# Decoder trunk on one core: 1 MB weight tiles, wider casts and evictions, and a new layout of the split tokens

## The chip, the cores and the metric

The kernel runs on one core of a Trainium2 chip. The metric is the time of one execution on the device in microseconds (us). Before the change its median over three runs is 2126.35 us (2126.17 to 2127.8). One execution more was profiled; its trace is what the sections below read. TensorE, VectorE and ScalarE are called PE, DVE and ACT in the trace's rows, PEld is TensorE's loading of stationary operands, and SP issues the transfers of weights.

## The reference

Two decoder layers over 256 tokens of width 2048, all in fp32. The first layer mixes tokens with a sparse attention (an indexer of 16 small heads scores the keys, the best 64 are kept for each query, then 16 heads in 4 groups share 4 key/value heads), the second with an mLSTM of 8 heads. Each is followed by a feed-forward part (FFN) of width 8192 with a squared ReLU.

```python
for i in range(DEPTH):                       # 2
    hn = rms_norm(h, norm_mix[i])
    if i % N_MIXERS == 0:
        y = dsa_attention(hn, att_w_in[j], att_q_gain[j], att_k_gain[j], att_w_out[j])
    else:
        y = mlstm_mixer(hn, ml_w_in[j], ml_b_gate[j], ml_h_gain[j], ml_w_out[j])
    h = h + y
    hn = rms_norm(h, norm_ffn[i])
    h = h + jnp.square(jax.nn.relu(hn @ ffn_w_up[i])) @ ffn_w_down[i]
```

## The kernel before

Nearly all of the work is products of the 256 tokens with weights of 389 MB in total, each read once. To keep fp32's precision on a faster matmul, every operand is split into a high part (the value cast to the type fp32r) and a low part (the value less its high part), and a product is the sum of high x high, high x low and low x high. The split of a tile is `split` (L134 to 136): a cast on ScalarE (L135), then a subtraction on VectorE (L136).

`weights` (L138) brings four blocks of 128 weight rows, a *group*, against at most 512 columns, in two halves. For each half it takes a tile `w` (five of them), one transfer of 512 KB (L144), a tile `wh` and a tile `wl` (four each), and splits the 1024 columns. So there is room for two groups in wh and wl, in steps of half a group.

`project` (L152) puts the tokens on the stationary side and the weights on the moving side: 24 matmuls of 512 columns for a group, in the lines L166 (high, high), L167 (high, low) and L168 (low, high). It serves the attention's and mLSTM's projections and FFN down. `project_t` (L175) has the weights stationary and the tokens moving, so that the result comes out transposed: per block and 128 columns one matmul of the high weights with the tokens' high and low parts side by side (L191, 512 columns) and one of the low weights with the tokens' high parts (L193, 256 columns). It serves FFN up and the mLSTM's q and k. Its results lie alternately in the tiles `acc` and `acx`.

A `pair` (L60) holds the two parts of two blocks of tokens: [part][block][256 tokens]. L191 therefore reads two runs of 256 elements that lie 512 apart. Pairs are written by `Norm.chunk` (xT, L226 and L227), by the attention (oT), the mLSTM (hsT) and the eviction of FFN up (hT).

FFN runs in four quarters of 2048 hidden columns: four times `project_t` (512 columns each) and then four times `project`. The eviction `evac_up` of FFN up takes one block of 128 hidden columns at a time: a copy (L462), a sum (L463), max and square (L464) and a split, all 256 wide.

The attention projects V, the indexer, K and then Q in four head groups. The indexer's scores go through L355 and L360, the top-k through L366 and L367; in a head group the logits (L412, L417), exponentials (L422) and scalings (L427) make probabilities `lg`, which TensorE transposes (L434 to 436), ScalarE copies to `pT` (L438) and TensorE multiplies with V (L440, L442).

Nobody writes the order of the engines' instructions out by hand. The program names work in order of its stages, and a scheduler that plays the program through with its own estimates of durations gives each engine a fixed sequence when the kernel is built; a tile of a pool is handed on when its last reader is done. A changed size therefore changes the sequences too. The tile numbers in the sequences below are those of the build.

## Time and profile before

| what | value |
|---|---|
| median of three runs | 2126.35 us |
| span of the profiled execution | 2124.9 us |
| TensorE busy | 2115.0 us, 10748 matmuls |
| VectorE busy | 1242.6 us (58%), 1866 instructions |
| ScalarE busy | 1010.1 us (48%), 1400 instructions |
| read from memory | 389.16 MB, 184 GB/s over the span |
| mean granted clock of TensorE | 0.999 |

The stages follow one another: attention up to about 282 us and its output projection to 330, FFN of the first layer to 1034, mLSTM, and FFN of the second layer from about 1420 to the end. A quarter of an FFN takes 176 us. "Busy" on TensorE is from a matmul's start to its modelled end, and as matmuls overlap in the pipeline, their pace is read better from how many of them run in a stretch. A share of the chain that ended last says how much of the span went by on that chain in this line's work; what waits beside it costs nothing.

### The profile page before, as it was taken

The numbers are of one execution on the slowest core, as the hardware profiler recorded it, in microseconds if no ns is written. First come the engines' busy times: TensorE is split into PE (matmuls) and PEld (weight loads), VectorE is DVE, ScalarE is ACT, GpSimd is POOL, SyncE is SP. The second block draws the span as 40 slices with busy tenths as digits, with TensorE's granted clock in tenths as the row PEclk, the third lists the DMA queues.
The fourth block names the chain that finished last, engine by engine and source line by source line (L and its number), as shares of the span: only waits on it lengthen the run. The fifth ranks groups of instructions, "written<-read, shape, count | busy, mean of one in ns | idle before, by whom it ended". The sixth has DMA issues, their size and how long they took to land.

```text
span 2124.9 us, 27918 instructions
## 1 busy us (share of the span) xinstructions
PE 2115.0 (100%) x10748; PEld 1810.0 (85%) x10748; DVE 1242.6 (58%) x1866; ACT 1010.1 (48%) x1400; POOL 14.0 (1%) x20
## 2 busy tenths in 40 slices
PE   9999999999999999999999999999999999999999
PEld 8988888888888888888999888888888888888887
DVE  5697656645555565565654565656555555654654
ACT  6556554534443443444554554545434434443542
POOL 0000000000000000000011000000000000000000
PEclk9999999999999999999999999999999999999999
DMA  7665356656656656665566555466566666666664
GB/s 234 188 180 151 119 178 188 188 193 191 191 191 187 198 189 196 190 189 188 166 185 209 171 165 176 161 188 188 193 194 189 191 194 189 191 193 191 189 205 140
DMA packets 207926, 393.09 MB, mean 185 GB/s; under 512 B 12784, under 2 KB 29616, under 8 KB 207792
## 3 DMA queue, kind: packets, MB, share of 16 engines
q1 hardware_dynamic: 207744, 391.29, 60.4%
q8 instruction: 84, 1.38, 0.2%
q14 instruction: 50, 0.41, 0.1%
q10 hardware_dynamic: 48, 0.02, 0.0%
HBM read 389.16 MB, written 2.10 MB: 184 GB/s over the span
## 4 chain that ended last, share of the span: by engine, by line
PE 99%; ACT 0%; DMA 0%; DVE 0%; issue 0%; SPq 0%; DVEq 0%
PE acc L167 19%; PE acc L168 19%; PE acc L166 19%; PE acc L191 13%; PE acx L191 13%; PE acc L193 6%; PE acx L193 6%; PE aux L219 1%; PE aux L412 0%; PE aux L440 0%; PE aux L620 0%; PE aux L349 0%; DMA w<-in_att_w_in_dram 0%; PE aux L611 0%; PE aux L396 0%; PE aux L645 0%
## 5 line engine op out<-in xcount | busy, mean ns | idle before, releaser
L136 DVE TENSOR_TENSOR wl<-w,wh 128x1024 fp32r<-128x1024 f32 (+3 forms) x752 | 907.1, 1207 | 820.6 <-ACT wh L135 819.5
L135 ACT CAST wh<-w 128x1024 fp32r<-128x1024 f32 (+3 forms) x752 | 777.6, 1035 | 970.6 <-PE acc L168 576.6
L191 PE MATMUL acc<-xT,wh 128*128 128x512 f32 x1152 | 401.1, 394 | 0.0
L191 PE MATMUL acx<-xT,wh 128*128 128x512 f32 x1152 | 399.9, 393 | 0.0
L166 PE MATMUL acc<-wh,hT 128*128 128x512 f32 x1024 | 398.7, 389 | 0.0
L167 PE MATMUL acc<-wl,hT 128*128 128x512 f32 x1024 | 398.7, 389 | 0.0
L168 PE MATMUL acc<-wh,hT 128*128 128x512 f32 x1024 | 398.4, 389 | 0.0
L193 PE MATMUL acc<-xT,wl 128*128 128x256 f32 x1152 | 318.9, 278 | 0.0
L193 PE MATMUL acx<-xT,wl 128*128 128x256 f32 x1152 | 318.4, 278 | 0.0
L191 PEld LDWEIGHTS acx<-xT,wh 128*128 128x128 f32 x1152 | 215.7, 187 | 49.3
L191 PEld LDWEIGHTS acc<-xT,wh 128*128 128x128 f32 x1152 | 215.4, 188 | 48.9
L166 PEld LDWEIGHTS acc<-wh,hT 128*128 128x128 f32 x1024 | 192.2, 188 | 40.0
L168 PEld LDWEIGHTS acc<-wh,hT 128*128 128x128 f32 x1024 | 192.2, 188 | 39.7
L167 PEld LDWEIGHTS acc<-wl,hT 128*128 128x128 f32 x1024 | 192.2, 188 | 39.5
L193 PEld LDWEIGHTS acc<-xT,wl 128*128 128x128 f32 x1152 | 216.5, 188 | 1.3
L193 PEld LDWEIGHTS acx<-xT,wl 128*128 128x128 f32 x1152 | 216.2, 188 | 0.3
L166 PE MATMUL acc<-wh,xT 128*128 128x512 f32 (+3 forms) x576 | 212.4, 372 | 2.3 <-ACT xT L226 2.3
L167 PE MATMUL acc<-wl,xT 128*128 128x512 f32 (+3 forms) x576 | 212.7, 371 | 0.0
L168 PE MATMUL acc<-wh,xT 128*128 128x512 f32 (+3 forms) x576 | 211.9, 371 | 0.0
L166 PEld LDWEIGHTS acc<-wh,xT 128*128 128x128 f32 x576 | 108.1, 188 | 15.1 <-ACT xT L226 2.5
L167 PEld LDWEIGHTS acc<-wl,xT 128*128 128x128 f32 x576 | 108.3, 188 | 12.9 <-issue 0.7
L168 PEld LDWEIGHTS acc<-wh,xT 128*128 128x128 f32 x576 | 108.3, 188 | 12.8 <-issue 0.3
(204 smaller groups left out, 1308.1 us busy)
## 6 DMA issues: line engine op xcount, KB each, us to landing
w<-in_ffn_w_up_dram SPq DMA_DIRECT2D x256, 512.0 KB, 3.8
w<-in_ffn_w_down_dram SPq DMA_DIRECT2D x256, 512.0 KB, 4.3
w<-in_ml_w_in_dram SPq DMA_DIRECT2D x64, 512.0 KB, 3.8
w<-in_att_w_in_dram SPq DMA_DIRECT2D x48, 512.0 KB, 4.4
w<-in_att_w_out_dram SPq DMA_DIRECT2D x32, 512.0 KB, 4.4
w<-in_ml_w_out_dram SPq DMA_DIRECT2D x32, 512.0 KB, 3.7
w<-in_ml_w_in_dram SPq DMA_DIRECT2D x32, 412.0 KB, 3.7
w<-in_att_w_in_dram SPq DMA_DIRECT2D x24, 368.0 KB, 3.6
```

The source lines that it names most:

```text
L135: nc.scalar.copy(hi, src)
L136: nc.vector.tensor_tensor(lo, src, hi.bitcast(F32), op=ALU.subtract)
L166: nc.tensor.matmul(o, ah, wh[:, j, :width], start=(k == 0), stop=False)
L167: nc.tensor.matmul(o, ah, wl[:, j, :width], start=False, stop=False)
L168: nc.tensor.matmul(o, al, wh[:, j, :width], start=False, stop=(k == nk - 1))
L191: nc.tensor.matmul(acc[j], wh[:, kk % 2, js], a[:, :, k % 2], start=(k == 0), stop=False, skip_group_check=True)
L193: nc.tensor.matmul(acc[j][:, 1], wl[:, kk % 2, js], a[:, 0, k % 2], start=False, stop=(k == nk - 1), skip_group_check=True)
L219: nc.tensor.transpose(p[:, j * T + m * P:j * T + (m + 1) * P], h[:, m, k * P:(k + 1) * P], ident)
```

## The change

1. `weights` takes one tile `w` of 1 MB for a group (three of them), one transfer of 1 MB, one wh and one wl of 2048 columns (two of each), one cast and one subtraction. Only the first projection, whose tokens are made on the way (`before`), keeps two pieces, inside the same tiles.
2. A `pair` is laid out [block][part][256 tokens], so the moving operand of L191 is one run of 512; all writers and readers of pairs follow.
3. `evac_up` collects two blocks in `u` and then does max and square and the split for both at once, 512 wide, with a tile `y` more.
4. The attention has one tile `sq` (was two) and four `lg` (was five); two small mLSTM tiles share others' space. Comments and docstrings go.

```diff
@@ weights
-    def weights(src, k0, n0, width):
-        parts = []
-        for i in range(2):
-            w = wp.tile([P, 2, 512], F32, tag="w", name=uid("w"), bufs=5)
-            r0 = k0 + 256 * i
-            nc.sync.dma_start(w[:, :, :width], src[r0:r0 + 256, n0:n0 + width].rearrange("(k p) f -> p k f", p=P))
-            wh = wp.tile([P, 2, 512], F32R, tag="wh", name=uid("wh"), bufs=4)
-            wl = wp.tile([P, 2, 512], F32R, tag="wl", name=uid("wl"), bufs=4)
-            split(wh[:, :, :width], wl[:, :, :width], w[:, :, :width])
-            parts.append((wh, wl))
-        return parts
+    def weights(src, k0, n0, width, pieces=1):
+        w = wp.tile([P, 4, 512], F32, tag="w", name=uid("w"), bufs=3)
+        wh = wp.tile([P, 4, 512], F32R, tag="wh", name=uid("wh"), bufs=2)
+        wl = wp.tile([P, 4, 512], F32R, tag="wl", name=uid("wl"), bufs=2)
+        n = 4 // pieces
+        for i in range(pieces):
+            r0 = k0 + 128 * n * i
+            ks = slice(n * i, n * (i + 1))
+            nc.sync.dma_start(w[:, ks, :width],
+                              src[r0:r0 + 128 * n, n0:n0 + width].rearrange("(k p) f -> p k f", p=P))
+            split(wh[:, ks, :width], wl[:, ks, :width], w[:, ks, :width])
+        return wh, wl
@@ project
-            for i, (wh, wl) in enumerate(weights(src, k0 + 512 * g, n0, width)):
+            wh, wl = weights(src, k0 + 512 * g, n0, width, 1 if before is None else 2)
+            for i in range(2):
...
-                        ah, al = a[:, 0, j, ms], a[:, 1, j, ms]
-                        nc.tensor.matmul(o, ah, wh[:, j, :width], start=(k == 0), stop=False)
-                        nc.tensor.matmul(o, ah, wl[:, j, :width], start=False, stop=False)
-                        nc.tensor.matmul(o, al, wh[:, j, :width], start=False, stop=(k == nk - 1))
+                        ah, al = a[:, j, 0, ms], a[:, j, 1, ms]
+                        hi, lo = wh[:, 2 * i + j, :width], wl[:, 2 * i + j, :width]
+                        nc.tensor.matmul(o, ah, hi, start=(k == 0), stop=False)
+                        nc.tensor.matmul(o, ah, lo, start=False, stop=False)
+                        nc.tensor.matmul(o, al, hi, start=False, stop=(k == nk - 1))
@@ project_t
-                a = lhs[k // 2]
+                a = lhs[k // 2][:, k % 2]
...
-                    nc.tensor.matmul(acc[j], wh[:, kk % 2, js], a[:, :, k % 2], start=(k == 0), stop=False,
-                                     skip_group_check=True)
-                    nc.tensor.matmul(acc[j][:, 1], wl[:, kk % 2, js], a[:, 0, k % 2], start=False,
-                                     stop=(k == nk - 1), skip_group_check=True)
+                    nc.tensor.matmul(acc[j], wh[:, kk, js], a, start=(k == 0), stop=False, skip_group_check=True)
+                    nc.tensor.matmul(acc[j][:, 1], wl[:, kk, js], a[:, 0], start=False, stop=(k == nk - 1),
                                      skip_group_check=True)
@@ Norm.chunk
-                    nc.scalar.activation(a[:, 0, j], src, AF.Copy, scale=g)
-                    nc.vector.scalar_tensor_tensor(a[:, 1, j], src, g, a[:, 0, j].bitcast(F32),
+                    nc.scalar.activation(a[:, j, 0], src, AF.Copy, scale=g)
+                    nc.vector.scalar_tensor_tensor(a[:, j, 1], src, g, a[:, j, 0].bitcast(F32),
@@ attention (mlstm's hsT alike)
-        slab = slabs(pool, {"v": 1, "kT": 1, "qT": 3, "hn": 3, "sq": 2, "ropa": 1, "ropb": 1, "lg": 5, "pT": 3, "sc": 4})
+        slab = slabs(pool, {"v": 1, "kT": 1, "qT": 3, "hn": 3, "sq": 1, "ropa": 1, "ropb": 1, "lg": 4, "pT": 3, "sc": 4})
...
-                split(a[:, 0], a[:, 1], po.rearrange("p (k t) -> p k t", k=2))
+                split(a[:, :, 0], a[:, :, 1], po.rearrange("p (k t) -> p k t", k=2))
@@ ffn
-            hT = []
+            hT, half = [], []
             def evac_up(b, p):
                 if b % 2 == 0:
-                    hT.append(pair("hT"))
-                a = hT[-1]
-                u = t2k([P, 2, T], F32, "u")
-                nc.scalar.copy(u[:, 0], p[:, 1])
-                nc.vector.tensor_tensor(u[:, 0], p[:, 0], u[:, 0], op=ALU.add)
-                nc.vector.scalar_tensor_tensor(u[:, 1], u[:, 0], 0.0, u[:, 0], op0=ALU.max, op1=ALU.mult)
-                split(a[:, 0, b % 2], a[:, 1, b % 2], u[:, 1])
+                    half.append(t2k([P, 2, T], F32, "u"))
+                u = half[-1]
+                nc.scalar.copy(u[:, b % 2], p[:, 1])
+                nc.vector.tensor_tensor(u[:, b % 2], p[:, 0], u[:, b % 2], op=ALU.add)
+                if b % 2 == 0:
+                    return
+                y = t2k([P, 2, T], F32, "y")
+                nc.vector.scalar_tensor_tensor(y, u, 0.0, u, op0=ALU.max, op1=ALU.mult)
+                a = pair("hT")
+                split(a[:, :, 0], a[:, :, 1], y)
+                hT.append(a)
@@ mlstm
-        gT = slab([MH, 2, T], "gT")
+        gT = slab([MH, 2, T], "gT", "mkT")
-        row = slab([MH, 2, T], "row")
+        row = slab([MH, 2, T], "row", "mqT")
```

The lines move by one to five: L191 and L193 become L193 and L194, L166 to 168 become L169 to 171, L438 becomes L439, L440 L441.

The first place is ScalarE in the softmax of the first head group: L422 are the exponentials, L135 the casts of weights, L438 (then L439) the copy of the transposed probabilities that TensorE waits for. Before:

```order
134 L135 CAST wh_1916<-w_1914 128x1024
135 L135 CAST wh_1922<-w_1920 128x1024
136 L422 ACTIVATE lg_1494,smx_1499<-lg_1494,mx_1495 128x256 x2
137 L135 CAST wh_1952<-w_1950 128x1024
138 L135 CAST wh_1958<-w_1956 128x1024
139 L438 COPY pT_1511<-aux_1507 128x384
140 L135 CAST wh_2136<-w_2134 128x1024
141 L135 CAST wh_2142<-w_2140 128x1024
```

And with the change:

```order
107 L423 ACTIVATE lg_1347,smx_1352<-lg_1347,mx_1348 128x256 x2
108 L135 CAST wh_1747<-w_1746 128x2048
109 L423 ACTIVATE lg_1362,smx_1367<-lg_1362,mx_1363 128x256 x2
110 L135 CAST wh_1777<-w_1776 128x2048
111 L439 COPY pT_1379<-aux_1375 128x384
112 L439 COPY pT_1387<-aux_1383 128x384
113 L135 CAST oT_1391<-aux_1374 128x2x256
```

Four half casts stand before the copy in the one, of which the last two come after the last exponentials; in the other two whole ones, the second of them next to the copy.

The second is TensorE at the same place: L434 to 436 (then L435 to 437) transpose the probabilities, L440 and L442 (L441 and L443) multiply their copy pT with V, the rest are a Q projection's matmuls. Before:

```order
803 L166 MATMUL acc_1841<-wh_1922,xT_258 128x512
804 L167 MATMUL acc_1841<-wl_1923,xT_258 128x512
805 L168 MATMUL acc_1841<-wh_1922,xT_258 128x512
806 L166 MATMUL acc_1840<-wh_1952,xT_306 128x512
807 L440 MATMUL aux_1506<-pT_1511,v_124 128x256
808 L442 MATMUL aux_1506<-pT_1511,v_124 128x128
809 L434 MATMUL aux_1515<-ident,lg_1458 128x128
810 L435 MATMUL aux_1515<-ident,lg_1479 128x128
```

And with the change:

```order
777 L169 MATMUL acc_1685<-wh_1717,xT_197 128x512
778 L170 MATMUL acc_1685<-wl_1718,xT_197 128x512
779 L171 MATMUL acc_1685<-wh_1717,xT_197 128x512
780 L435 MATMUL aux_1375<-ident,lg_1326 128x128
781 L436 MATMUL aux_1375<-ident,lg_1347 128x128
782 L437 MATMUL aux_1375<-ident,lg_1347 128x128
783 L169 MATMUL acc_1684<-wh_1747,xT_242 128x512
784 L169 MATMUL acc_1685<-wh_1747,xT_242 128x512
785 L441 MATMUL aux_1374<-pT_1379,v_124 128x256
786 L443 MATMUL aux_1374<-pT_1379,v_124 128x128
787 L435 MATMUL aux_1383<-ident,lg_1326 128x128
```

The first three transposes, which aux_1507 takes before, stand 25 weight matmuls ahead of the L440 that uses their copy; with the change those of aux_1375 stand two matmuls ahead of it, and L171 just before them is the last reader of wh_1717, the tile that the cast of wh_1777 takes over.

The third is TensorE at the start of a group of FFN up (its weights wh_3346 and wl_3347, then wh_3015 and wl_3016). Before:

```order
1546 L191 MATMUL acx_3340<-xT_2575,wh_3346 128x512
1547 L193 MATMUL acx_3340<-xT_2575,wl_3347 128x256
1548 L191 MATMUL acx_3341<-xT_2575,wh_3346 128x512
1549 L193 MATMUL acx_3341<-xT_2575,wl_3347 128x256
1550 L191 MATMUL acx_3342<-xT_2575,wh_3346 128x512
1551 L193 MATMUL acx_3342<-xT_2575,wl_3347 128x256
```

And with the change:

```order
1547 L193 MATMUL acx_3010<-xT_2347,wh_3015 128x512
1548 L193 MATMUL acx_3011<-xT_2347,wh_3015 128x512
1549 L193 MATMUL acx_3012<-xT_2347,wh_3015 128x512
1550 L193 MATMUL acx_3013<-xT_2347,wh_3015 128x512
1551 L194 MATMUL acx_3010<-xT_2347,wl_3016 128x256
1552 L194 MATMUL acx_3011<-xT_2347,wl_3016 128x256
1553 L194 MATMUL acx_3012<-xT_2347,wl_3016 128x256
1554 L194 MATMUL acx_3013<-xT_2347,wl_3016 128x256
1555 L193 MATMUL acx_3010<-xT_2347,wh_3015 128x512
1556 L194 MATMUL acx_3010<-xT_2347,wl_3016 128x256
```

High and low matmuls alternated from the first on; now the four high ones of the group's first block come first, the four low ones follow, and only from the second block on do they alternate.

## Rows read from the trace of the kernel before

**Rows 1.** The page: busy us by engine; the chain that ended last.
```profile
PE 2115.0 (100%) x10748; PEld 1810.0 (85%) x10748; DVE 1242.6 (58%) x1866; ACT 1010.1 (48%) x1400; POOL 14.0 (1%) x20
...
PE 99%; ACT 0%; DMA 0%; DVE 0%; issue 0%; SPq 0%; DVEq 0%
```

**Rows 2.** Waits of TensorE: line, waited for, us in total, times, longest.
```profile
PE aux L440 <- ACT pT L438: 2.2, 2, 2.0
...
PE acc L167 <- DVE wl L136: 0.4, 1, 0.4
```

**Rows 3.** Table by stage: length, busy us (count) by engine, clock, DMA share.
```profile
46.00:160.00 114.00, 114.00 (x613) 99.43 (x612) 83.95 (x193) 61.48 (x84) 0.00 (x0) 1.00 0.64 184
...
160.00:282.00 122.00, 119.40 (x595) 100.37 (x594) 82.90 (x244) 70.86 (x143) 0.15 (x2) 1.00 0.43 135
...
506.60:682.40 175.80, 175.80 (x898) 149.65 (x897) 99.22 (x120) 77.56 (x96) 0.00 (x0) 1.00 0.62 192
```

**Rows 4.** The same table for L191 alone, then for L168 alone.
```profile
510.00:590.00 80.00, 80.00 (x231) 43.23 (x232) 1.00 0.63 190
...
600.00:680.00 80.00, 45.61 (x118) 21.96 (x117) 1.00 0.62 195
```

**Rows 5.** Chain of waits (start, us, what): FFN up, then mLSTM's output projection.
```profile
1259.91 0.93 PE acx L191 x4
...
1260.84 0.47 PE acx L193 x4
...
1353.35 0.46 PE acc L166 x2
```

**Rows 6.** By line and shape (busy, mean ns): subtractions, then casts.
```profile
L136 DVE TENSOR_TENSOR wl<-w,wh 128x1024 fp32r<-128x1024 f32 x688 | 842.5, 1225 | 759.6 <-ACT wh L135 759.1
...
L136 DVE TENSOR_TENSOR hT<-u,hT 128x256 fp32r<-128x256 f32 x128 | 48.3, 420 | 0.0
...
L136 DVE TENSOR_TENSOR wl<-w,wh 128x736 fp32r<-128x736 f32 x24 | 22.1, 926 | 24.7 <-ACT wh L135 24.6
...
L135 ACT CAST wh<-w 128x1024 fp32r<-128x1024 f32 x688 | 723.2, 1052 | 907.8 <-PE acc L168 521.1 <-PE acc L191 180.9 <-PE acx L191 167.6
...
L135 ACT CAST wh<-w 128x736 fp32r<-128x736 f32 x24 | 19.3, 809 | 23.1 <-PE acc L168 18.2 <-issue 4.1 <-ACT xT L226 0.8
```

**Rows 7.** Timeline of FFN down (start, us, instruction, [idle before <-releaser]).
```profile
630.30 0.39 PE L168 MATMUL acc<-wh,hT 128*128 128x512 f32 x1
...
630.73 1.05 ACT L135 CAST wh<-w 128x1024 fp32r<-128x1024 f32 x1 [1.66 <-PE acc L168]
...
631.82 1.23 DVE L136 TENSOR_TENSOR wl<-w,wh 128x1024 fp32r<-128x1024 f32 x1 [1.49 <-ACT wh L135]
```

**Rows 8.** Timeline of VectorE in the top-k.
```profile
97.15 5.53 DVE L360 SCALAR_TENSOR_TENSOR score<-rl,wi,score 128x128 f32<-128x128 f32 x14
...
104.11 0.29 DVE L366 MAX8 top<-score 128x8 f32<-128x128 f32 x1
...
108.84 1.22 DVE L136 TENSOR_TENSOR wl<-w,wh 128x1024 fp32r<-128x1024 f32 x1
```

**Rows 9.** Timeline of ScalarE, then TensorE, third head group.
```profile
231.67 1.04 ACT L135 CAST wh<-w 128x1024 fp32r<-128x1024 f32 x1
...
232.93 1.04 ACT L135 CAST wh<-w 128x1024 fp32r<-128x1024 f32 x1 [0.23 <-ACT wh L135]
...
233.88 0.50 ACT L422 ACTIVATE lg<-lg,mx 128x256 f32<-128x256 f32 x1
...
234.88 0.45 ACT L438 COPY pT<-aux 128x384 f32<-128x384 f32 x1
...
232.46 0.39 PE L168 MATMUL acc<-wh,oT 128*128 128x512 f32 x1
...
235.39 0.70 PE L440 MATMUL aux<-pT,v 128*128 128x256 f32 x2 [1.99 <-ACT pT L438]
```

**Rows 10.** The page: weight loads, KB each, median us to landing.
```profile
w<-in_ffn_w_up_dram SPq DMA_DIRECT2D x256, 512.0 KB, 3.8
```

More of the change, by code (lines that the diff above doesn't have):

```diff
@@ L183, in project_t @@
         for g in range(nk // 4):
-            parts = weights(src, 512 * g, n0, 512)
+            wh, wl = weights(src, 512 * g, n0, 512)
             for kk in range(4):
                 k = 4 * g + kk
-                wh, wl = parts[kk // 2]
-                a = lhs[k // 2]
+                a = lhs[k // 2][:, k % 2]
                 for j in range(4):
                     js = slice(j * P, (j + 1) * P)
-                    nc.tensor.matmul(acc[j], wh[:, kk % 2, js], a[:, :, k % 2], start=(k == 0), stop=False,
+                    nc.tensor.matmul(acc[j], wh[:, kk, js], a, start=(k == 0), stop=False, skip_group_check=True)
+                    nc.tensor.matmul(acc[j][:, 1], wl[:, kk, js], a[:, 0], start=False, stop=(k == nk - 1),
                                      skip_group_check=True)
-                    nc.tensor.matmul(acc[j][:, 1], wl[:, kk % 2, js], a[:, 0, k % 2], start=False,
-                                     stop=(k == nk - 1), skip_group_check=True)
         for b in range(4):
@@ L486, in mlstm @@
     def mlstm(nm, nxt, pool):
-        slab = slabs(pool, {"go": 4, "mkT": 1, "mqT": 1, "mv": 2, "num": 2, "gT": 1, "row": 1, "et": 2, "pt": 2,
+        slab = slabs(pool, {"go": 4, "mkT": 1, "mqT": 1, "mv": 2, "num": 2, "et": 2, "pt": 2,
                             "mjunk": 2, "hs": 3})
@@ L647, in mlstm @@
                     t = pair("hsT")
-                    split(t[:, 0], t[:, 1], pT.rearrange("p (k t) -> p k t", k=2))
+                    split(t[:, :, 0], t[:, :, 1], pT.rearrange("p (k t) -> p k t", k=2))
                     hsT.append(t)
```

## The prediction

> **What bounds the kernel now.** I read the page's busy shares and its chain that ended last first: TensorE is busy for 2115.0 us of the 2124.9 us span, and 99% of the chain is its own matmuls [rows 1]. So a time saved elsewhere counts only where TensorE waits, and the table of waits, read next, shows how little of that there is: beside the start, 2.2 us in the attention (L440 for pT) and 0.4 us for a low part of the weights (L167 for wl) [rows 2]. The table by stage says where the others have room: in a feed-forward quarter (506.6 to 682.4) VectorE works 99.2 and ScalarE 77.6 of 175.8 us, in the first attention stretch (46 to 160) VectorE 84 of 114 us, in the second 83 of 122 us, and there TensorE first loses time, 2.6 us [rows 3]. What can move the time is thus the pace of TensorE's matmuls, and whether the split weights (cast to wh, subtraction to wl) still reach it in time.
>
> **The pace: contiguous token parts.** L191 has two runs of 256 elements as its moving operand and gets one of 512. In 80 us of FFN up 231 of them run, each with an L193 of 256 columns: 80/231 = 346 to 347 ns for a pair. In FFN down, where the moving operand is contiguous, 118 of L168 run in 80 us, one of three equal lines: 80/(3 x 118) = 226 ns [rows 4]. Four L191 behind one another take 0.93 us, 232 ns each, four L193 0.47 us, 118 each; two L166, contiguous, take 0.46 us, 230 each [rows 5]. So the second run costs from 232.5 - 230 = 2.5 ns to 232.5 - 226 = 6.5 ns if it costs anything at all, and nothing if the gap comes from the alternating 512- and 256-wide results. With 2304 L191 (two groups of 1152) the gain lies between 0 and 15 us. I take 3.5 ns, between the two contiguous rows: 2304 x 3.5 = **-8 us**. The new sequence also puts four high and then four low matmuls at each group's start; by those rows 0.93 + 0.47 = 1.40 us against 4 x 0.347 = 1.39, so that costs nothing.
>
> The page SBUF — State Buffer of the Trainium skill, Specifications (TRN2), says that at least two hits in a 16-byte cacheline give full bandwidth. By it a run of 256 fp32 is as good as one of 512 and the gain would be nothing; the trace's 232 against 226 to 230 ns leans the other way, though it can't tell the layout from the result widths.
>
> **The large tiles on ScalarE and VectorE.** A cast of 1024 columns takes 1052 ns and one of 736 809 ns: 0.84 ns a column, so one of 2048 takes 1.05 + 0.86 = 1.92 us. A subtraction takes 1225 and 926 ns: 1.04 ns a column, so 2.29 us [rows 6]. Two casts cost 2.10 us, two subtractions 2.45: some 0.18 us of ScalarE and 0.16 us of VectorE go per group of four k-blocks, and the wider FFN evictions free a little more (256 columns take 420 ns, where 1.04 ns a column would be 266). All of this is on engines with 77 us idle or more in a quarter, so it is worth nothing by itself.
>
> What counts is the wait. Both before and after, two groups of wh and wl exist, but before they are freed and filled in halves (four tiles), after whole. The cast of the next group now can't begin before the last matmul of the group before last, and the last low part is ready only after cast and subtraction of all four blocks. From rows: last matmul L168 at 630.30, its cast at 630.73, 0.43 later; the cast ends at 631.78 and the subtraction starts at 631.82 [rows 7]. So a new group is ready 0.43 + 1.92 + 0.04 + 2.29 = 4.7 us after the last matmul that frees it. TensorE needs 24 x 0.226 = 5.4 us for a group of FFN down and 16 x 0.347 = 5.55 us for one of FFN up, and the first matmul(s) at a group's start take only wh (two in FFN down, four in FFN up), which adds 0.45 to 0.93 us. Margin: 1.1 us and 1.8 us. An eviction of FFN up that stands in between on VectorE fits (256 columns take 0.42 us [rows 6], twice that at most at double width). With casts and subtractions at twice the half's price the chain is 5.0 us, still hidden. FFN stages: **0**; above that there is only the rival of late groups. A 1 MB transfer takes the place of two of 512 KB, each landed after 3.8 us [rows 10]; three tiles leave two groups, some 11 us, for a load that took 3.8 to 4 us for each half even one after the other, and so it is covered.
>
> **Where the attention loses it.** VectorE there has long runs of other work between two subtractions.
> (a) *Top-k.* Before, 14 scores take 5.53 us (0.395 each), and from 104.11 to the next subtraction at 108.84 a chain of top-k and scores runs for 4.7 us [rows 8]. In the new order five scores (2.0 us) and a chain of twenty operations like it (4.7 us and up) stand between the subtractions of K's last group and Q's first, with the subtraction 9.0 us; 17 more such operations (some 5.5 us) precede the next, 7.8 us. TensorE takes 5.4 us for each of the two groups. The shortfall is 16.8 - 10.8 = 6.0 us, less the lead with which VectorE comes in: 1.1 us if it is the FFN's margin, up to all of it if VectorE is as far ahead there as before (its scores end at 102.7, and its next subtraction is early). I take **+3 us**, the middle of 0 to 6.
> (b) *First softmax.* ScalarE has CAST wh_1777 right ahead of COPY pT_1379, and TensorE's L441 stands only three transposes and two matmuls behind the last reader of the tile which that cast waits for. The copy is done 0.43 + 1.92 + 0.45 + 0.1 = 2.9 us after that reader begins, TensorE is there after 0.23 + 3 x 0.11 + 2 x 0.23 = 1.0: **+1.9 us**. (The copy's 0.45 is from rows 9; 0.1 for hand-overs and 0.11 for a transpose, a little under L193's 0.118, are estimates.) Before, 25 weight matmuls stand between the transposes and L440. Behind the waiting L441 is every weight matmul of the group.
> (c) *Third head group.* Before, ScalarE does two half casts (231.67, 232.93), two exponentials, then the copy at 234.88, and L440 waits 1.99 us for it until 235.39 [rows 9]. The one cast can now begin only where the second stood, since its tile is freed by the last matmul at 232.46: it ends at 234.85 instead of 233.97, which makes the copy 0.9 us late; the subtraction, whole behind the cast, ends 2.29 us later at 237.2, where its second half could end at 233.97 + 1.23 = 235.2, and the scaling of the last probabilities, next on VectorE, is up to 2 us later with it: together **+1.8 us**.
> (d) *Last head group.* The same with no matmul behind the transposes but two: cast, two exponentials (1.0 us, from 233.88 to 234.88), copy: 0.43 + 1.92 + 1.0 + 0.45 + 0.1 = 3.9 less 1.0 = 2.9, against the 0.4 us of waiting for wl before [rows 2]: **+2.5 us**.
> Sum 9.2 us. What I can't walk (the narrow tiles of 368 to 416 columns, the mLSTM's heads, where VectorE has one stretch of almost 5 us between subtractions) I bound by 0 and +5 and take **+2**, the size of the one place (c). The attention's sum I bound by +3 (leads absorb all but the last place) and +14 (each half as long again).
>
> The smaller slabs (sq, lg, and shared mLSTM tags) add waits on ScalarE and VectorE alone; none is nearer to TensorE than those above. Cost 0.
>
> **Sum:** -8 + 9.2 + 2 = +3.2. The profiled execution's span of 2124.9 us becomes 2128.1; it lies 1.4 us below the median of 2126.35, so the time is **2129.5 us**.
>
> **Rivals.** (1) *The pace wins.* One 512-wide run takes 227 ns and the scheduler's order leaves room: 2304 x 4.7 = -11 us, stalls +4: 2126 - 7 = 2119. For it: every contiguous row is below 232. Against it: the waits of (b) and (d) follow from fixed orders. (2) *Nothing from the layout, slower.* The alternating widths set 347 ns; gain 0, stalls +11 to +14: 2138. It decides as soon as the gain is under 2 ns a matmul. The cacheline rule above is on its side. (3) *Late groups.* Where the chain of 4.7 us turns out longer than the 5.9 us cover, by 1.2 us of queueing or slower wide operations, every group is late: 0.1 us each over the 256 FFN groups (256 halves of FFN up [rows 10] and as many of FFN down, two to a group) gives +26 us: 2150. Against it: both operations' prices are linear in rows 6. (4) *Two whole groups suffice everywhere*, so that the change does what its sizes say and only the pace is left: 2118, counted with (1).
>
> The page Trainium Kernel Development and Optimization of the Trainium skill (Best Practices) advises double buffering; that rule would have two whole tiles hide all, which is rival (4), and for the FFN the rows' margin of 1.1 us agrees, for the attention they don't.
>
> **How the numbers follow.** My forecast 0.45, with its own range 2124 to 2135; rivals (1) and (4) 0.32; (2) 0.17; (3) 0.06. A difference of 0.2% (4.25 us: 2122.1 to 2130.6) is about what can be told from no change. The forecast's part splits 0.02 faster, 0.28 same, 0.15 slower; (1) and (4) 0.29 faster, 0.03 same; (2) and (3) are slower. So 0.31, 0.31, 0.38. The range reaches into (1) and (2): 2114 to 2142.
>
> **What would show it.** The pair L193 + L194 in FFN up should run in 343 to 344 ns (some 233 of L193 in 80 us); at 347 the layout gives nothing. Casts of 2048 should take 1.9 and subtractions 2.3 us. In the table of waits L441 for pT should stand at 5 to 9 us, L170 for wl at 2 to 5, both inside 46 to 282; in the FFN quarters TensorE should stay busy throughout. Waits for wl or wh there, or a quarter over 176 us, would make me wrong to the slow side; attention stages no longer than 236 us between 46 and 282, to the fast side.

## The result and the profile after

The changed kernel takes **2163.52 us** (median of 4 runs, 2163.47 to 2163.56) against 2126.41: a ratio of 1.0172, 95% interval 1.0158 to 1.0187. It is slower by 37 us, 21.5 us above the range that was given. Its profiled execution spans 2161.7 us, 36.8 more than before.

The page of the changed kernel, the rows that answer to [rows 1]:

```profile
PE 2134.2 (99%) x10748; PEld 1819.4 (84%) x10748; DVE 1193.5 (55%) x1366; ACT 930.6 (43%) x964; POOL 11.9 (1%) x20
...
PE 96%; DVE 2%; ACT 1%; issue 0%; DMA 0%; SPq 0%; ACTq 0%; DVEq 0%
```

TensorE is still the chain, but 96% and not 99% of it; VectorE and ScalarE, which had none, now have 3%. TensorE's idle time grew from 9.9 us to 27.5, and its busy time by 19 us as well, though it does the same matmuls. So there are two losses: waits, and a slower pace. The table of TensorE's waits, which answers to [rows 2]:

```profile
PE acc L170 <- DVE wl L136: 7.8, 6, 1.6
PE aux L441 <- ACT pT L439: 3.9, 3, 1.7
PE acc L169 <- ACT wh L135: 3.3, 4, 2.0
PE acc L169 <- ACT xT L227: 2.6, 1, 2.6
PE aux L436 <- DVE lg L428: 2.3, 2, 1.2
PE acx L194 <- DVE wl L136: 1.1, 1, 1.1
PE aux L93 <- DVE zero L76: 1.0, 1, 1.0
PE acc L169 <- ACT oT L135: 0.4, 1, 0.4
PE aux L220 <- DVE h L269: 0.3, 1, 0.3
```

Against 5.9 us before it waits 22.7: for low and high parts of weights (wl, wh), for pT and for the scaled probabilities lg (the waits for xT and zero are at the start, as before). The next table is read from the timelines: the time in us from the first weight matmul of a stage to that of the next. "K, Q" is everything from the first weight matmul until the attention's output projection starts, "out A" that projection with the last heads, "up" the eight FFN up stages, "mLSTM" what lies between FFN and its output projection, "out M" that projection with its last heads. FFN down is 612.0 to 612.3 us for seven stages in every run and is left out. The rows below the second are the experiments.

| run | ratio to before [95%] | K, Q | out A | up | mLSTM | out M |
|---|---|---|---|---|---|---|
| before | | 205.6 | 112.3 | 712.2 | 285.6 | 96.8 |
| **after** | 1.0172 [1.0158, 1.0187] | 209.0 | 120.7 | 719.3 | 291.3 | 108.6 |
| e1_layout | 1.0000 [0.9990, 1.0009] | 205.9 | 112.3 | 712.2 | 285.6 | 96.8 |
| e2_tiles | 1.0165 [1.0149, 1.0180] | 208.8 | 122.1 | 719.3 | 291.2 | 106.0 |
| e3_evac | 1.0004 [0.9994, 1.0013] | 206.3 | 112.4 | 712.2 | 285.6 | 96.8 |
| e4_halves | 0.9998 [0.9988, 1.0007] | 206.0 | 113.5 | 712.2 | 285.6 | 96.8 |
| e5_pieces | 1.0060 [1.0045, 1.0075] | 206.0 | 119.2 | 715.6 | 287.2 | 100.2 |
| e6_first | 1.0028 [1.0018, 1.0038] | 205.6 | 112.4 | 719.0 | 286.0 | 96.8 |
| e7_all | 1.0037 [1.0024, 1.0050] | 206.8 | 113.7 | 719.8 | 285.6 | 96.8 |
| e8_wl | 1.0108 [1.0091, 1.0124] | 208.3 | 118.4 | 718.9 | 289.1 | 101.1 |
| e9_wh | 1.0059 [1.0044, 1.0074] | 206.2 | 115.7 | 721.1 | 285.0 | 98.1 |
| e10_snake | 1.0016 [1.0006, 1.0025] | 206.4 | 113.6 | 716.2 | 285.3 | 96.8 |
| e11_ring3 | 1.0071 [1.0054, 1.0087] | 209.6 | 116.9 | 714.3 | 286.6 | 101.1 |
| e12_stagger | 1.0045 [1.0030, 1.0060] | 206.8 | 113.7 | 722.2 | 285.6 | 96.8 |
| e13_unpin | 1.0081 [1.0066, 1.0096] | 209.3 | 116.1 | 719.3 | 291.2 | 95.0 |
| e14_before_unpin | 0.9992 [0.9983, 1.0002] | 205.3 | 111.1 | 712.2 | 285.6 | 96.8 |
| e15_unpin_pieces | 1.0027 [1.0017, 1.0036] | 206.9 | 114.6 | 715.6 | 287.2 | 95.0 |

So the 36.3 us between the first and last weight stage are: K, Q 3.4, out A 8.4, FFN up 7.1, mLSTM 5.7, out M 11.7. In this and what follows "outside FFN up" is the sum of the four others, 29.2 us.

Two things have to be known of this table. The borders are set by the sequence: in the changed kernel, e2_tiles, e5_pieces, e8_wl, e13_unpin and e15_unpin_pieces eleven more matmuls of the heads lie before the mLSTM's output projection than in the others, 1.1 to 1.4 us, which stand under "mLSTM" and are missing from "out M". Set right, the changed kernel loses about 4.4 us in the mLSTM and 13 in out M. (In e11_ring3 25 more lie before out A.) No sum over the stages is touched by it. And each row is one profiled execution: in those of e4_halves, e7_all, e10_snake and e12_stagger out A holds a short drop of TensorE's clock that those of before, e1_layout, e3_evac and e6_first don't have, and is 1.2 to 1.4 us longer by it.

**FFN up.** The prediction hoped for 344 ns a pair of high and low matmul. The timeline of TensorE in two neighbouring groups of a quarter (each row is the start of a step; between the first and second, and the third and fourth, lie 12 pairs):

```profile
700.17 0.40 PE L193 MATMUL acc<-xT,wh 128*128 128x512 f32 x1
...
704.41 1.09 PE L193 MATMUL acc<-xT,wh 128*128 128x512 f32 x4
...
705.81 0.40 PE L193 MATMUL acc<-xT,wh 128*128 128x512 f32 x1
...
709.98 1.09 PE L193 MATMUL acc<-xT,wh 128*128 128x512 f32 x4
```

704.41 - 700.17 = 4.24 us, 353 ns a pair; 709.98 - 705.81 = 4.17 us, 347 ns. Groups alternate between these two all the way through. Before, all pairs ran at 347 ns [rows 4], but for the first of each stage.

**The waits.** The chain of waits of the changed kernel in the mLSTM's output projection (start, us, what), where out M loses most:

```profile
1361.23 0.24 PE acc L171
1361.47 0.02 issue
1361.49 1.91 ACT wh L135
1363.39 0.02 issue
1363.42 2.30 DVE wl L136
1365.72 0.04 issue
1365.77 0.79 PE acc L170
1366.56 0.43 PE acc L171
...
1370.83 0.43 PE acc L170
1371.25 0.26 PE acc L171
1371.51 0.23 PE acc L169
```

The cast begins 0.26 us after the *last matmul before it* has begun, then comes the subtraction, then TensorE. It had two high matmuls to do in these 4.5 us. So nothing was in stock: the two tiles of wh served as one. And after the wait each matmul takes 0.43 us instead of 0.23, until 1371.25. The table by stretches (length, busy us (count) of PE, PEld, DVE, ACT and POOL, granted clock, DMA share, GB/s) shows why, here in the mLSTM and at two places of the attention:

```profile
1352.00:1360.00 8.00, 8.00 (x38) 6.71 (x37) 3.58 (x5) 3.91 (x8) 0.00 (x0) 1.00 0.37 131
1360.00:1368.00 8.00, 4.42 (x14) 2.96 (x13) 6.44 (x22) 2.80 (x5) 0.00 (x0) 0.77 0.50 157
1368.00:1376.00 8.00, 7.11 (x28) 5.28 (x26) 0.91 (x2) 2.36 (x3) 0.00 (x0) 0.80 0.27 106
236.00:244.00 8.00, 5.15 (x23) 3.75 (x22) 5.39 (x17) 5.30 (x14) 0.00 (x0) 0.84 0.16 42
256.00:264.00 8.00, 6.53 (x24) 5.09 (x25) 3.92 (x9) 3.07 (x7) 0.00 (x0) 0.79 0.39 130
```

The granted clock, as the mean of 8 us, is 0.77 to 0.84 where TensorE has just been idle for some us, between its two levels of 2.4 GHz and 1.2 GHz; the 0.43 us matmuls are those at 1.2. From 46 us on and but for the last few, what is missing to a clock of 1.00 adds up to 8.5 us (before: nothing), 5.1 of it in out M and 3.4 in out A. TensorE stood still for 1.8 us of these drops, so the clock costs some 7.6 us. With the 16.8 us by which the waits grew and FFN up's 7.1 that is 31.5 of the 36.8 us; the rest was not followed up.

### The profile page after: what moved, and what is told of

It reads as the page before. It is cut to its first block, busy times and chain, and to the rows that moved or that the text cites. A ratio compares the mean times of both kernels' runs of the same rounds, so it can differ in the third digit from the quotient of the medians.

```text
span 2161.7 us, 25510 instructions
## 1 busy us (share of the span) xinstructions
PE 2134.2 (99%) x10748; PEld 1819.4 (84%) x10748; DVE 1193.5 (55%) x1366; ACT 930.6 (43%) x964; POOL 11.9 (1%) x20
## 4 chain that ended last, share of the span: by engine, by line
PE 96%; DVE 2%; ACT 1%; issue 0%; DMA 0%; SPq 0%; ACTq 0%; DVEq 0%
PE acc L170 19%; PE acc L171 19%; PE acc L169 19%; PE acx L193 12%; PE acc L193 12%; PE acx L194 6%; PE acc L194 6%; DVE wl L136 1%; ACT wh L135 1%; PE aux L220 1%; PE aux L441 0%; PE aux L413 0%; PE aux L625 0%; ACT lg L423 0%; DMA w<-in_att_w_in_dram 0%
## 5 line engine op out<-in xcount | busy, mean ns | idle before, releaser
L136 DVE TENSOR_TENSOR wl<-w,wh 128x2048 fp32r<-128x2048 f32 (+4 forms) x380 | 850.3, 2238 | 808.9 <-ACT wh L135 808.7
L135 ACT CAST wh<-w 128x2048 fp32r<-128x2048 f32 (+4 forms) x380 | 706.3, 1859 | 936.5 <-PE acc L171 495.1
L171 PE MATMUL acc<-wh,hT 128*128 128x512 f32 x1024 | 398.4, 389 | 0.0
L193 PE MATMUL acc<-xT,wh 128*128 128x512 f32 x1152 | 385.6, 396 | 0.0
L193 PE MATMUL acx<-xT,wh 128*128 128x512 f32 x1152 | 382.8, 395 | 0.1
L169 PE MATMUL acc<-wh,hT 128*128 128x512 f32 x1024 | 378.2, 390 | 0.0
L194 PE MATMUL acc<-xT,wl 128*128 128x256 f32 x1152 | 291.8, 281 | 0.1
L194 PE MATMUL acx<-xT,wl 128*128 128x256 f32 x1152 | 289.0, 281 | 1.2 <-DVE wl L136 1.1
L193 PEld LDWEIGHTS acc<-xT,wh 128*128 128x128 f32 x1152 | 211.9, 188 | 45.0
L193 PEld LDWEIGHTS acx<-xT,wh 128*128 128x128 f32 x1152 | 211.1, 188 | 45.0 <-ACT wh L135 0.4
L171 PEld LDWEIGHTS acc<-wh,hT 128*128 128x128 f32 x1024 | 192.2, 188 | 40.0
L169 PEld LDWEIGHTS acc<-wh,hT 128*128 128x128 f32 x1024 | 191.6, 188 | 39.5
L194 PEld LDWEIGHTS acx<-xT,wl 128*128 128x128 f32 x1152 | 207.7, 189 | 8.0 <-DVE wl L136 2.1
L194 PEld LDWEIGHTS acc<-xT,wl 128*128 128x128 f32 x1152 | 208.9, 189 | 6.5 <-DVE wl L136 0.6
L171 PE MATMUL acc<-wh,xT 128*128 128x512 f32 (+3 forms) x576 | 212.2, 371 | 0.0
L169 PE MATMUL acc<-wh,xT 128*128 128x512 f32 (+3 forms) x576 | 202.5, 372 | 2.6 <-ACT xT L227 2.6
L169 PEld LDWEIGHTS acc<-wh,xT 128*128 128x128 f32 x576 | 107.4, 188 | 15.5 <-ACT xT L227 2.8
L171 PEld LDWEIGHTS acc<-wh,xT 128*128 128x128 f32 x576 | 108.2, 188 | 12.9 <-issue 0.7
```

Of the source, the lines that this page charges most:

```text
L135: nc.scalar.copy(hi, src)
L136: nc.vector.tensor_tensor(lo, src, hi.bitcast(F32), op=ALU.subtract)
L169: nc.tensor.matmul(o, ah, hi, start=(k == 0), stop=False)
L171: nc.tensor.matmul(o, al, hi, start=False, stop=(k == nk - 1))
L193: nc.tensor.matmul(acc[j], wh[:, kk, js], a, start=(k == 0), stop=False, skip_group_check=True)
L194: nc.tensor.matmul(acc[j][:, 1], wl[:, kk, js], a[:, 0], start=False, stop=(k == nk - 1), skip_group_check=True)
```

## The experiments

The two theories at the start: **whole tiles** (wh and wl handed on by groups bring the waits, and, by the order that follows from them, FFN up's pace) against **the other parts** (layout, evictions, 1 MB transfers, small slabs). The first four runs tell them apart.

**e1_layout** does part 2 of the change alone:

```diff
-  ... wh[:, kk % 2, js], a[:, :, k % 2] ...
+  ... wh[:, kk % 2, js], a[:, k % 2] ...
-  nc.scalar.activation(a[:, 0, j], src, AF.Copy, scale=g)
+  nc.scalar.activation(a[:, j, 0], src, AF.Copy, scale=g)
```

> The kernel before with the new layout of the token pairs alone (weights in halves and evictions as before; TensorE's sequence is as before, high and low matmuls alternating). The changed kernel's FFN up takes 89.7 us a quarter against 88.8, its groups alternately 347 and 352 ns a pair. Layout theory (one run of 512 is itself slower): FFN up 89.7 us, total 2126 + 8 x 0.9 = 2134. Order theory (the four high matmuls first at each group's start do it, the layout is worth nothing): FFN up 88.8, 2126 (2125 to 2128). The prediction's pace step: 344 instead of 347 ns, FFN up 88.0 or less, 2118.

Measured: 2127.5 us against 2127.25, FFN up to a tenth as before. The table by stage for L191 alone (compare [rows 4], 231 there):

```profile
510.00:590.00 80.00, 80.00 (x232) 43.23 (x232) 1.00 0.64 190
```

One run of 512 is as fast as two of 256, to less than 1 ns a matmul. This agrees with the cacheline rule of the Trainium skill's page SBUF — State Buffer (Specifications (TRN2)), which the prediction had put behind its own reading of 232 against 226 to 230 ns.

**e2_tiles** does part 1 alone (with part 4, for the space):

```diff
-            w = wp.tile([P, 2, 512], F32, tag="w", name=uid("w"), bufs=5)
+        w = wp.tile([P, 4, 512], F32, tag="w", name=uid("w"), bufs=3)
-            wh = wp.tile([P, 2, 512], F32R, tag="wh", name=uid("wh"), bufs=4)
+        wh = wp.tile([P, 4, 512], F32R, tag="wh", name=uid("wh"), bufs=2)
```

> The kernel before with the whole-group weight tiles alone (one 1 MB transfer, one cast, one subtraction; with them the smaller slabs that the space asks for); layout and evictions as before. TensorE's sequence now starts nearly every FFN up group with four high, then four low matmuls. Whole-tile theory (waits come from handing on wh and wl by whole groups, with the clock drops that follow): the attention and mLSTM lose 25 to 30 us as in the changed kernel, whatever the layout. With the order theory FFN up takes 89.7 us a quarter too: total 2160 to 2165. With the layout theory FFN up stays at 88.8: total 2153 to 2157. Rival (the evictions or the layout cause the waits too): under 2145.

2163.05 us: the whole loss, FFN up's part included.

**e3_evac** does part 3 alone (the new `evac_up`, written to the old layout):

```diff
-                nc.vector.scalar_tensor_tensor(u[:, 1], u[:, 0], 0.0, u[:, 0], op0=ALU.max, op1=ALU.mult)
-                split(a[:, 0, b % 2], a[:, 1, b % 2], u[:, 1])
+                nc.vector.scalar_tensor_tensor(y, u, 0.0, u, op0=ALU.max, op1=ALU.mult)
+                split(a[:, 0], a[:, 1], y)
```

> The kernel before with the eviction of FFN up for two blocks at once alone. Both theories: off TensorE's path, 2126 within 2 us. A rival (the longer eviction delays the next group's subtraction): FFN up longer than 88.8 us by some tenths, 2128 to 2134.

2128.03 against 2127.25: nothing that can be told from no change.

**e4_halves** is the changed kernel with wh and wl as before, cut from the 1 MB tile:

```diff
-        wh = wp.tile([P, 4, 512], F32R, tag="wh", name=uid("wh"), bufs=2)
-        wl = wp.tile([P, 4, 512], F32R, tag="wl", name=uid("wl"), bufs=2)
+            wh = wp.tile([P, 2, 512], F32R, tag="wh", name=uid("wh"), bufs=4)
+            wl = wp.tile([P, 2, 512], F32R, tag="wl", name=uid("wl"), bufs=4)
+            split(wh[:, :, :width], wl[:, :, :width], w[:, ks, :width])
```

> The changed kernel with wh and wl in halves again (four tiles each, casts and subtractions of 1024); the 1 MB transfer, the layout, the evictions and the small slabs stay. Whole-tile theory: waits of TensorE back to 6 us and no clock drops, with the order theory FFN up at 88.8: total 2126 to 2129. Layout theory: FFN up stays at 89.7, total 2133 to 2136. Rival (the 1 MB transfers or the smaller slabs make the waits): 2145 or more.

2127.09: all is back. The layout, the evictions, the 1 MB transfers and the small slabs together are worth nothing either way (K, Q is 0.4 us longer; out A is 1.2 longer, with the drop of the clock that the table's note names). The loss is in whole wh and wl tiles alone.

The next four ask what it is about them: the width of the operations, the hand-over, or the order of matmuls.

**e5_pieces**: whole tiles, but transfers, casts and subtractions in halves:

```diff
-            wh, wl = weights(src, k0 + 512 * g, n0, width, 1 if before is None else 2)
+            wh, wl = weights(src, k0 + 512 * g, n0, width, 2)
...
-            wh, wl = weights(src, 512 * g, n0, 512)
+            wh, wl = weights(src, 512 * g, n0, 512, 2)
```

> The changed kernel with transfers, casts and subtractions in halves (512 KB, 1024 columns) inside the whole-group tiles w, wh and wl, which are still two each and handed on whole. TensorE's sequence alternates high and low from the group's start again. Hand-over theory (a whole tile is freed only by its group's last matmul): waits stay near the changed kernel's, +15 us or more outside FFN up. Width theory (a single operation of 2048 columns holds back the first low part and the other work of ScalarE and VectorE): back to 2126 to 2131. For FFN up: order theory 88.8 us, address theory (the place of whole tiles) 89.7.

2141.37. Neither theory alone: outside FFN up 12.3 us are left of 29.2. They lie nearly all in the two output projections: with the border set right K, Q keeps 0.4 us and the mLSTM 0.5, out A 6.9 and out M 4.5. FFN up is 88.84 us in six of its eight stages, against 88.80 before; the first stage of each FFN is 1.6 us longer, and in it the pairs run at 353 ns from the second group on, though the sequence is the same.

**e6_first**: the kernel before, with the four high matmuls first in each group's first block, as the whole tiles make the order:

```diff
+                if kk == 0:
+                    for j in range(4):
+                        high(j)
+                    for j in range(4):
+                        low(j)
+                else:
+                    for j in range(4):
+                        high(j)
+                        low(j)
```

> The kernel before with one edit in the order of FFN up's and mLSTM's matmuls: in the first block of each group the four high ones come first, then the four low ones. Weights, layout, evictions as before. Order theory: FFN up 89.7 us a quarter, its groups alternately 347 and 352 ns a pair; 8 x 0.9 us plus 1.6 in the mLSTM: 2134 to 2136. Address theory: 2127, FFN up 88.8.

2134.55, FFN up 719.0: the order alone is enough to make FFN up's loss.

**e7_all**: the same in every block.

```diff
+                for j in range(4):
+                    high(j)
+                for j in range(4):
+                    low(j)
```

> The kernel before with four high and then four low matmuls in every block of FFN up and of the mLSTM's q and k. If the cost sits in the block itself (four high, four low take 20 ns more than four pairs, from the pitches of the changed kernel's trace: 4 x (233.3 + 119.1) against 4 x 347.5), FFN up takes 64 x 0.02 = 1.3 us more, 90.1, total 2137 to 2139. If it sits in the pairs behind such a block (every second group at 352 ns), there are no pairs left to be slow: at most 89.0, total 2126 to 2129.

2136.79, FFN up 89.76 us a stage: 15 ns a block, of 20 expected. So in e6_first 16 such blocks cost 0.24 us of the 0.84, and the rest comes from the pairs behind them: 8 groups of 12 pairs at 6 ns make 0.58.

**e8_wl**: the changed kernel with wl alone in halves (two subtractions), wh whole.

```diff
-        wl = wp.tile([P, 4, 512], F32R, tag="wl", name=uid("wl"), bufs=2)
+        wl = [wp.tile([P, 2, 512], F32R, tag="wl", name=uid("wl"), bufs=4) for _ in range(2)]
```

> The changed kernel with wl alone in halves (four tiles, subtractions of 1024); wh stays whole (two tiles, casts of 2048). Width theory: the first low part comes 1.1 us earlier and VectorE's work is cut finer, but ScalarE's copies still stand behind casts of 1.9 us: half of the 22 us of waits goes, 2140 to 2150. Hand-over theory: the cast still waits for the whole group before last, so most of it stays: 2150 to 2160. If low parts alone are what TensorE waits for: under 2136.

2150.92; outside FFN up 16.6 us are left.

**e9_wh**: the other way round, wh in halves (casts and subtractions of 1024), wl whole.

```diff
-        wh = wp.tile([P, 4, 512], F32R, tag="wh", name=uid("wh"), bufs=2)
+        wh = [wp.tile([P, 2, 512], F32R, tag="wh", name=uid("wh"), bufs=4) for _ in range(2)]
```

> The changed kernel with wh in halves (four tiles), casts and subtractions of 1024; wl stays whole (two tiles). The counterpart of the run with wl in halves, and beside the run with two pieces in whole tiles (2141) it differs only in that wh is freed by halves. If the hand-over of wh is what kept 13 us there, under 2132; if that of wl does it too, as both are freed by the same matmuls but for one, 2136 to 2143. FFN up at 88.8, as high and low alternate.

2141.45, but for a reason that no theory had: outside FFN up only 4.7 us are left, so of e5_pieces' 12.3 the hand-over of wh makes 7.6 (the transfers differ too, 1 MB here and 512 KB there, but e4_halves found no price for that), while FFN up, in which high and low alternate plainly, is slower than in any run before. Its timeline (12 pairs between the rows):

```profile
541.29 0.40 PE L196 MATMUL acx<-xT,wh 128*128 128x512 f32 x1
...
545.53 0.40 PE L196 MATMUL acx<-xT,wh 128*128 128x512 f32 x1
```

353 ns a pair, in one group after another, in six of the eight stages; the other two, the first of each FFN, run at 347. That is e5_pieces the other way round, with the same alternation. So the order is not the cause by itself: pairs of alternating widths have more than one steady rhythm, and four high matmuls in a row are one thing that changes it. That whatever comes just before decides which rhythm follows is a guess that no run isolates.

**e10_snake** and **e12_stagger** try whether another order runs faster than that of before: every second pair turned round, and each low matmul one block late, so that neighbours add into different result tiles.

```diff
+                    if j % 2 and 0 < k:
+                        low(j, False)
+                        high(j, k == nk - 1)
...
+                    low()
+                    late.append((k, j, wl, a))
```

The first three lines are e10_snake's, the last two e12_stagger's: there `low()` does the low matmul that the step before has put into `late`.

> The kernel before with every second pair of matmuls of FFN up and of the mLSTM's q and k turned round (high low, low high), so that two matmuls of one kind follow one another half of the time. If what costs is each block's break in a steady high-low alternation, every block has it and FFN up is slower, 89.5 us or more, total 2133 to 2138. If a high matmul right after another costs nothing and each change of width costs time, it has half the changes and gains: 88.0, 2120.

> The kernel before with each low matmul of FFN up and of the mLSTM's q and k behind the high one of the next block of 128 columns, so high and low still alternate but two neighbours never add into the same result tile. If the 231.8 and 115.7 ns of before come from neighbours that share a result tile, pairs fall to 341 to 344 ns and FFN up to 87.5 to 88.0: 2119 to 2123. If they come from the change of widths, nothing moves: FFN up 88.8, 2126 to 2128.

2131.1 and 2137.88, FFN up 716.2 and 722.2 against 712.2: slower in both. e12_stagger runs at 353 ns a pair in three of the four blocks of 512 columns of each stage and at 347 in the first. These are the two paces of e9_wh, whose neighbours do share a result tile, so no cost of sharing is seen.

**e11_ring3**: the kernel before with three halves instead of four, its operations as before.

```diff
-            wh = wp.tile([P, 2, 512], F32R, tag="wh", name=uid("wh"), bufs=4)
-            wl = wp.tile([P, 2, 512], F32R, tag="wl", name=uid("wl"), bufs=4)
+            wh = wp.tile([P, 2, 512], F32R, tag="wh", name=uid("wh"), bufs=3)
+            wl = wp.tile([P, 2, 512], F32R, tag="wl", name=uid("wl"), bufs=3)
```

> The kernel before with three half tiles of wh and of wl instead of four; all operations stay as before (1024 columns). Hand-over theory, from the other side: a half is freed one half later, so its chain of 2.75 us has 2.7 us less cover; waits of several us come in the attention's and mLSTM's busy stretches, with clock drops, and half the FFN up groups begin with high matmuls: 2134 to 2150. Width theory alone (only large operations hurt): 2127 to 2130.

2142.68: with nothing wide in it, 13.9 us are lost outside FFN up. The stock of finished weights was what kept the kernel before nearly free of waits.

By then it was open why two whole groups are so much less stock than four halves. The sequence of TensorE in the changed kernel answers (hsT_9200 are heads that are done, hsT_9972 the last heads):

```
6558 L171 MATMUL acc_10136<-wh_10138,hsT_8991 128x512
...
6563 L169 MATMUL acc_10135<-wh_10168,hsT_9200 128x512
...
6565 L169 MATMUL acc_9987<-wh_10080,hsT_9972 128x512
```

wh_10080 is the last group of the first 512 output columns. Tiles are dealt out in the program's order, so it is cast before wh_10138 and wh_10168, but its heads come late, and it is used after them. It *pins* one of two tiles; the other groups have the second alone. Four halves leave two for them. The casts of wh_10080, wh_10138 and wh_10168 in the trace:

```profile
1354.72 1.91 ACT L135 CAST wh<-w 128x2048 fp32r<-128x2048 f32 x1 [1.61 <-PE acc L171]
...
1361.49 1.90 ACT L135 CAST wh<-w 128x2048 fp32r<-128x2048 f32 x1 [0.56 <-PE acc L171]
1373.64 1.90 ACT L135 CAST wh<-w 128x2048 fp32r<-128x2048 f32 x1 [10.26 <-PE acc L171]
```

wh_10080 is ready at 1356.6 and first used at about 1376; in between the other two casts wait each for the last matmul of the group just before. Three runs test it.

**e13_unpin**: the changed kernel, with that group asked for later in both output projections.

```diff
-        for c in range(4):
-            project(hsT, w_mo, 0, 512 * c, 512, at(c))
+        project_two(hsT, w_mo, at)     # columns 0 to 1023
+        for c in (2, 3):
+            project(hsT, w_mo, 0, 512 * c, 512, at(c))
...
+        for c, g in ((0, 0), (0, 1), (0, 2), (1, 0), (1, 1), (1, 2), (0, 3), (1, 3)):
```

> The changed kernel with one edit in the two output projections: the last group of output columns 0 to 511 is asked for behind the first three groups of columns 512 to 1023, so that in the mLSTM no group takes a tile while its heads are missing. Pinning theory: the mLSTM's output projection falls from 108.6 us to 97 to 99, and the clock no longer drops in it; the attention keeps most of its loss, since there the third group is still taken early; total 2150 to 2155. Ring-depth or width theory: 106 to 109 us there, total 2160 to 2165.

2145.66: out M falls from 108.6 to 95.0 us (with the border set right, from some 110 to 96.3, against 96.8 before). Its table by stretches, at the place that had the clock of 0.77:

```profile
1360.00:1368.00 8.00, 8.00 (x40) 6.70 (x39) 5.65 (x11) 2.04 (x2) 0.00 (x0) 1.00 0.42 136
1368.00:1376.00 8.00, 8.00 (x38) 6.57 (x37) 3.84 (x5) 4.77 (x4) 0.00 (x0) 1.00 0.58 205
```

TensorE is busy throughout, at 1.00. Out A, where the third group is still taken early, keeps 3.8 of its 8.4 us, but its clock no longer drops either, so the total came out 4 us under the expectation.

**e15_unpin_pieces** adds the halved operations (its edit is that of e13_unpin and e5_pieces together), **e14_before_unpin** puts the same `project_two` into the kernel before.

> The changed kernel with the new order of groups and transfers, casts and subtractions in halves inside the whole tiles (2141 without the new order). Pinning theory: the mLSTM's output projection falls from 100.2 us to 97 to 98; with FFN up alternating from the start 88.8: total 2134 to 2138, the rest in the attention. Ring-depth theory: no change, 2141.

> The kernel before with the same order of groups in the output projections. With four half tiles a group that waits leaves two halves, enough for the chain of 2.75 us, so there is little to gain: 2125 to 2128, the mLSTM's output projection at 96.8 us. If the order is worth something by itself (fewer waits in the attention as well): 2122 to 2124.

2133.53: 3.4 us are left outside FFN up (3.4 more in FFN up). Of 29.2 us, the new order of groups alone takes 17.9, the halved operations alone 16.9, both 25.8. They do not act at the same places. The halved operations alone bring back K, Q and the mLSTM but for 0.9 us; the new order alone leaves 3.7 and some 4.3 us there, but brings back all of out M and half of out A. So the long chain of cast and subtraction, 4.5 us, is what costs the projections with two free tiles, and in the output projections the pinned group lays it bare once more; that is where the two overlap, by 9.0 us. e14_before_unpin, 2126.08 against 2127.24, has its interval across 1; no run is clearly faster than the kernel before.

## Why the prediction was wrong

- **The pace, -8 us: failed, +7.1.** The step took 232 against 226 to 230 ns for the price of a second run. e1_layout shows 0 for it. The same paragraph set the new order (four high, four low) at nothing, from two averages, 1.40 against 1.39 us: the block itself costs 15 ns, 1.402 against 1.387, and the sum could not show that it changes the rhythm of the twelve pairs behind it. This is 15.1 of the 33 us by which the sum was off. A quarter takes 176.8 us, over the 176 that the prediction named as a sign against it.
- **"Two groups of wh and wl exist": failed.** That is so in the FFN, where groups are used in the order in which they are asked for, and there the step was right: FFN down 87.07 against 87.05 us, and the operations as worked out from [rows 6] (1.92 and 2.29 us; by line and shape, subtraction and cast):

```profile
L136 DVE TENSOR_TENSOR wl<-w,wh 128x2048 fp32r<-128x2048 f32 x340 | 780.8, 2297 | 736.8 <-ACT wh L135 736.8
...
L135 ACT CAST wh<-w 128x2048 fp32r<-128x2048 f32 x340 | 649.4, 1910 | 878.5 <-PE acc L171 444.8 <-issue 216.7 <-PE acc L193 131.2
```

  In both output projections one group is pinned, and the two groups are one. The term for the mLSTM and the rest, +2, measured 5.7 + 11.7 = 17.4: 15.4 us off, most of it out M. The prediction had walked the attention's sequence, and bounded the mLSTM by the places where VectorE is long between subtractions; in out M it is not VectorE's length that counts but that no tile is free (e13_unpin).
- **The attention, +9.2: 11.8 measured, a total that is nearer than its parts.** Place (b) came nearly as worked out; the chain of waits there:

```profile
175.56 0.24 PE acc L171
175.80 0.02 issue
175.82 1.90 ACT wh L135
177.72 0.39 ACT pT L439
178.11 0.04 issue
178.15 0.70 PE aux L441 x2
```

  The cast begins 0.26 us after the reader's start, not 0.43, and L441 waits 1.6 us, of 1.9 forecast. The wait behind the top-k (a) is 1.4 us, of 3. In (c) and (d) TensorE waits 4.9 us against 2.6 before, so 2.3 more, of 4.3. The four places thus gave 5.3 of 9.2 us. Two waits that were not forecast, 0.4 us at 227.1 and 1.4 us at 280.8, add 1.8, and the clock, which falls twice in out A, up to 3.4; 1.3 us are left open. That the total came within 3 us is luck.
- **The clock was left out.** The drops behind waits miss 8.5 us of clock in the changed kernel, and the prediction priced every wait by its own length alone. Its trace gave it no price: behind the longest wait of the kernel before outside the start, 2.0 us until 235.39, the clock stayed at 1.00. But that was one execution; in the profile of e7_all, with the same wait until 236.64, it fell (e7_all, then before):

```profile
236.00:244.00 8.00, 7.36 (x36) 6.34 (x37) 2.15 (x5) 3.58 (x9) 0.00 (x0) 0.79 0.40 131
236.00:244.00 8.00, 7.76 (x51) 6.80 (x50) 1.06 (x3) 4.21 (x8) 0.00 (x0) 1.00 0.38 125
```

  e4_halves, e10_snake and e12_stagger show it too, while e13_unpin waits 10.6 us outside the start and its clock never falls there. So a wait's price by the clock is not its length times a factor.
- **Evictions, transfers and slabs, 0: right** (e3_evac, e4_halves).
- **The rivals.** (1) fell with the pace. (2) had the right side and the right reading of the layout, at a third of the size. (3), late groups in all FFN stages, did not come (its +26 us on 2126 would also have been 2152, not 2150). (4) is what the pinned group refutes.

## What to carry to other kernels

Count a ring of tiles by what is free at the worst moment, not by its length: walk the places where a tile is handed out in program order but used late, since there a ring of two is a ring of one, and finer tiles of the same bytes keep a second. Larger operations on engines off the path pay nothing and lengthen the chain from a freed tile to the next finished one; halving them gave back 16.9 of 29.2 us here, about as much as the order did. Before a gain is read from some ns of pitch, the pitch should be seen in two arrangements of the same sizes.

## What was unexpected of the hardware

- Alternating matmuls of 512 and 256 columns have more than one steady rhythm: 347 ns a pair in the kernel before, 353 ns in three quarters of e12_stagger's FFN up, and both in turn in the changed kernel. The same alternation ran at either: e5_pieces at 353 in the first stage of each FFN (91.3 us) and at 347 in the other six (88.84), e9_wh at 347 in the first (89.7) and at 353 in the others (90.28). Both paces occur with the old layout and with the new, and with neighbours that share a result tile as with such that don't; what picks the rhythm was not found. Before was in the faster one.
- Around 1361 us TensorE stood still for 3.6 us within 4.3, and then did 13 matmuls of 512 columns in 5.6 us at half its clock, where 13 take 3.0 at full: a stall of 3.6 us cost about 6.2. A wait of 2.0 us was followed by such a drop in the profiles of four runs and by none in those of four others.
